# A conformer block with dilated attention: the place of one small DMA read in SyncE's queue

## The chip, the cores and the metric

The kernel runs on one core of one Trainium2 chip. The metric is the device time in microseconds (us) of one execution; the lower the better. Engines are named as the profile names them: PE is TensorE, DVE is VectorE, ACT is ScalarE, POOL is GpSimd, and SP is SyncE, which here does nothing but issue DMAs.

## The reference

One block on a sequence of 1024 tokens of width 1024: a gated convolution branch and an attention branch are mixed by gates and projected, and a feed-forward part with a short convolution follows. Only the attention matters here. Each of the 16 heads attends three times, with windows of 128, 512 and 2048 tokens at dilations 1, 4 and 16, and the three results are mixed by their log-sum-exp:

```python
for window, dilation in DILATION_GROUPS:          # (128, 1), (512, 4), (2048, 16)
    o_g, lse_g = dilated_window_attention(q, k, v, slopes, window, dilation)
    outs.append(o_g)
    lses.append(lse_g)
mix = jax.nn.softmax(jnp.stack(lses), axis=0)
o = jnp.einsum('gbsh,gbshd->bshd', mix, jnp.stack(outs))
```

That is one softmax over all (query, key) pairs with a bias: -slope x distance plus the logarithm of how many of the three windows hold the pair.

## The kernel before, in words

The kernel runs through stages: input norm and convolution branch, query-key-value projection, gate products, the **attention loop**, output projections, feed-forward part. The attention loop takes the stretch from about 590 to 864 us.

**Heads and slots.** A head is eight steps ("places" 0 to 7), two halves of four. Places 0 to 3 score the first 512 queries. Places 4 to 7 score the last 512 queries, in two parts: the *far* keys (more than the near range away, taken by residue modulo 4, place 4) and the *near* keys (query blocks 7, 6, then 4 and 5, at places 5 to 7). A score goes to PSUM (L924, L925, L963), VectorE adds the mask and takes the row's extreme (L928), ScalarE takes the exponential and sums it (L972). Twelve steps later the weights are transposed on PE (`flip`, L1023), split into a high and a low part on ACT and DVE (`ph` L1044, `pl` L1045), and multiplied with the values (`weigh`, L1061, L1062). Between these, PE works on the gate and convolution projections (L120 to L122), which fill its time.

**The statistics.** For the last 512 queries the far part and the near part of a row's softmax are computed apart, in different partition layouts. Each has a pair (extreme, sum) per row, kept in the tile `own[h]`: index 0 on its second axis is near, 1 is far. To join them, each side must see the other's pair in its own layout, in the tile `other[h]`:

- `near_to_far(h)` (L989) copies the near pairs to the far layout, four DMAs of 1 KB from SBUF to SBUF, one for each near query block. Each needs that block's sum.
- `far_out(h)` (L992) writes the far pairs, 4 KB, to a DRAM buffer `dstat[h % 2]`.
- `far_to_near(h)` (L995) reads them back in the near layout, 4 KB. It must wait until the write has landed.
- `compare(h)` (L999) subtracts the two extremes on VectorE. It is the first reader of `other` and needs all five copies. `combine(h)` follows one step later: the common factor (L1005 to L1008) and the scaling of the weights on POOL (L975).

By the program, for head h: `far_out` comes at place 6, `near_to_far` at place 0 of the next head, `far_to_near` at place 1 of the next head, `compare` at place 5 of the next head.

**The loads.** `head(h)` (L741 to L750) loads for one head the queries `q` and the keys `kk` (two DMAs), 512 KB each, and the mask `m`, 320 KB. Each tile has two buffers. `head(h + 2)` is called at place 1 of head h + 1, in the same step as `far_to_near(h)` and before it. `values(h)` loads `v` and `vf`.

**What sets the order.** PE, DVE, ACT and POOL run the loop in the order written (a manual schedule). SyncE is not among them: a scheduler puts its DMAs into one queue by its own estimate of when each is ready. SyncE issues strictly in that order; a DMA that waits holds all behind it. In the order that the scheduler made, the read `far_to_near(h)` stands right behind its write `far_out(h)`, or one DMA later. Outputs that pass through the same queue: `do` (the head's result, L1072), `dgate` and `dya` (L234, L249), and loads of weights and convolution rows `raw_*` (L93).

Of the kernel before, what the change touches and what calls it, by code (L numbers as in the profile page):

```python
# [61 lines left out]
def block_kernel(ctx: ExitStack, tc: tile.TileContext, x, xT, x0, g2, pack, mask,  # L62
                 w_first, w_ch, w_qkv, w_co, w_ao, w_o, w_up, w_down, out):
    nc = tc.nc
    act, dve, pool, pe, sp = nc.scalar, nc.vector, nc.gpsimd, nc.tensor, nc.sync
# [88 lines left out]
    def fetch(dst, src):  # L154
        sp.dma_start(dst.bitcast(F32), src.bitcast(F32))
# [12 lines left out]
    dstat = [dr.tile([P, 4, 2], F32, name=f"dstat{i}") for i in range(2)]  # L168
# [137 lines left out]
    if True:  # L306
# [156 lines left out]
        a, b = range(4), range(4, 8)  # L463
# [269 lines left out]
        def conv_result(c):  # L733
# [4 lines left out]
                           scale=pk[:, C_CG + c : C_CG + c + 1])  # L738
            act.dma_start(da[:, c, :], ordered)

        def head(h):  # L741
            hp, r, g8 = h // 2, (h % 2) * DH, h // 8
            q = p2.tile([P, T], F32R, tag="q", bufs=2, name=f"q_{h}")
            kk = p2.tile([P, 2, T], F32R, tag="kk", bufs=2, name=f"kk_{h}")
            m = p2.tile([P, 640], F32, tag="m", bufs=2, name=f"m_{h}")
            fetch(q, dq[g8].rearrange("p s c t -> (p s) c t")[2 * r : 2 * r + P, hp % 4, :])
            for s in range(2):
                fetch(kk[s:P:2], dk[g8][r : r + DH, :, hp % 4, :])
            sp.dma_start(m, mask[h])
            return q, kk[:, 0], kk[:, 1], m  # L750

        cover(COVER)
# [65 lines left out]
        with tc.manual_schedule(engines=hand):  # L818
# [4 lines left out]
            for n, (a, b) in enumerate(PAIRS):  # L823
# [13 lines left out]
                if n == 3:  # L837
                    tiles[0] = head(0)
# [57 lines left out]
    if True:  # L896
# [84 lines left out]
        own, other, shares = {}, {}, {}  # L981
# [4 lines left out]

        def near_to_far(h):
            for i in range(4):
                sp.dma_start(other[h][32 * i : 32 * i + 32, 1], own[h][:, 0, i])  # L989

        def far_out(h):
            sp.dma_start(dstat[h % 2], own[h][:, 1])  # L992

        def far_to_near(h):
            sp.dma_start(other[h][:, 0], dstat[h % 2].rearrange("(i a) r s -> (a r) i s", i=4))  # L995

        def compare(h):
            f = ready2("both", [P, 2, 4], F32, 2, f"both_{h}")
# [111 lines left out]
        with tc.manual_schedule(engines={ENG.Activation, ENG.DVE, ENG.PE, ENG.Pool}):  # L1110
# [3 lines left out]
            for at in range(len(slots) + BACK + 1):  # L1114
# [4 lines left out]
                if cur is not None:  # L1119
                    h, half, n = cur  # L1120
                    place = at % 8
                    if place == 4:
                        statistics(h)
                    if place == 5:
                        values(h)
                    if place == 1 and h + 1 < H:
                        tiles[h + 1] = head(h + 1)
                    new = score(h, tiles[h], SCORES[half][n])
# [27 lines left out]
                for ago, n0, send in ((2, 0, far_out), (1, 3, near_to_far), (READ, 0, far_to_near)):  # L1156
                    if 0 <= at - ago < len(slots) and slots[at - ago][1:] == (1, n0):
                        send(slots[at - ago][0])
# [343 lines left out]
    if True:  # L1502
# [49 lines left out]
        for f in range(FT):  # L1552
# [12 lines left out]
            r = ready.pop(0)  # L1565
# [15 lines left out]
    with tc.tile_pool(name="ph5", bufs=1, reuse_waits="tile") as p5_:  # L1581
# [31 lines left out]
        def residual(half, n, j):  # L1613
            r = p5_.tile([P, 512], F32, tag="res", bufs=4, name=f"res_{half}_{n}_{j}")
            sp.dma_start(r, dx2[half * 4 + n][:, j * 512 : j * 512 + 512])
            return r
# [107 lines left out]
        for n in range(3):  # L1724
            r = residual(0, n, 1)
# [75 lines left out]
```

## Time and profile before

| | |
|---|---|
| median of 3 runs | 1699.01 us (1698.5 to 1700.75) |
| the profiled execution: its own time | 1695.4 us |
| the profiled execution: span, first to last instruction | 1693.6 us |
| granted TensorE clock | 1.000 |
| attention loop | 590 to 864 us |
| one head in the loop | 16.1 to 18.9 us from one comparison (L999) to the next |

How to read the rows that the prediction shows. A row of the timeline is: start, duration, engine, line, operation, output tile <- input tiles, shape, count, and in brackets the idle time of that engine before it and what ended it. For SyncE (SPq) a row is the issue of a DMA, not its transfer. The view of waits gives total, times and longest. The name of the one that ended a wait is inferred: where several DMAs are waited for, it can name another than the one that came last. The view by windows gives, for a stretch, each engine's busy time, the clock and the DMA engines' share. "DMA to landing" is the time from issue until the data has landed, as minimum, median and maximum of the instructions chosen.

### The profile page before, as it was taken

Reading aid. Unit: us, or ns where it says so; the run is one execution under the profiler, and the core shown is the slowest. Engines: PE = TensorE matmul, PEld = TensorE weight load, DVE = VectorE, ACT = ScalarE, POOL = GpSimd, SP = SyncE. Lnnn points to the kernel's source line nnn. Section 1 sums busy time; section 2 is a strip of 40 time slices with the busy share of each in tenths; the row PEclk is TensorE's granted clock in tenths of the full one; section 3 lists DMA queues with packets and bytes.
Section 4 is the critical chain, followed back from the end, with each engine's and each line's share of the span. In section 5 each row is a group of like instructions: output and inputs, shape, how many; then the busy total and the mean of one; then the engine's idle time right before and its main releaser. Section 6 shows DMA issues by size and latency. Waiting matters only on the chain.

```text
span 1693.6 us, 22622 instructions
## 1 busy us (share of the span) xinstructions
PE 1681.4 (99%) x7939; PEld 1397.1 (82%) x7939; DVE 1303.1 (77%) x2114; ACT 787.9 (47%) x1351; POOL 224.3 (13%) x300
## 2 busy tenths in 40 slices
PE   9999999999999999999999999999999999999999
PEld 7888888888888888888888888888888888888887
DVE  6999999999876567767658654887777677789863
ACT  5411233233245478767646433544544455543431
POOL 0000132033000255555410000000000000000000
PEclk9999999999999999999999999999999999999999
DMA  9411145344555977886769594622222222499851
GB/s 375 153 50 50 50 137 162 125 137 137 175 178 195 320 226 238 261 243 201 221 214 333 187 335 147 227 99 76 75 90 85 87 75 87 145 366 322 287 172 50
DMA packets 187121, 300.24 MB, mean 177 GB/s; under 512 B 32256, under 2 KB 90240, under 8 KB 186496
## 3 DMA queue, kind: packets, MB, share of 16 engines
q1 hardware_dynamic: 185712, 294.48, 52.1%
q10 hardware_dynamic: 1296, 4.33, 0.6%
q8 instruction: 62, 1.02, 0.2%
q14 instruction: 51, 0.42, 0.1%
HBM read 214.74 MB, written 83.95 MB: 176 GB/s over the span
## 4 chain that ended last, share of the span: by engine, by line
PE 92%; DMA 3%; DVE 2%; ACT 1%; issue 1%; SPq 0%; POOL 0%; ACTq 0%; DVEq 0%
PE dx L1607 7%; PE xz L144 6%; PE xz L145 6%; PE xz L146 6%; PE dy L1607 5%; PE qkv L139 5%; PE qkv L137 5%; PE qkv L138 5%; PE y L145 2%; PE y L144 2%; PE y L146 2%; PE pp L1023 2%; PE wo L138 2%; PE wo L139 2%; PE wo L137 2%; PE o L1062 2%
## 5 line engine op out<-in xcount | busy, mean ns | idle before, releaser
L137 PE MATMUL qkv<-hi_qkv,hT 128*128 128x512 f32 x384 | 151.2, 395 | 0.0
L139 PE MATMUL qkv<-hi_qkv,hT 128*128 128x512 f32 x384 | 149.8, 391 | 0.0
L138 PE MATMUL qkv<-lo_qkv,hT 128*128 128x512 f32 x384 | 149.8, 391 | 0.0
L1510 DVE SCALAR_TENSOR_TENSOR u<-u,pk 128x1023 f32<-128x1023 f32 x88 | 112.1, 1275 | 1.2 <-ACT u L1508 0.9
L113 POOL TENSOR_TENSOR rs<-ss,mhalf 128x8 f32<-128x8 f32 x32 | 66.3, 2074 | 294.0 <-DVE ss L112 294.0
L1045 DVE TENSOR_TENSOR pl<-pp,ph 128x512 fp32r<-128x512 f32 (+1 forms) x95 | 58.7, 618 | 46.7 <-ACT ph L1044 46.5
L586 DVE SCALAR_TENSOR_TENSOR cacc<-csum,both,cacc 128x512 f32<-128x512 f32 x120 | 89.4, 745 | 0.3
L586 DVE SCALAR_TENSOR_TENSOR cacc<-apad,pk,cacc 128x512 f32<-128x512 f32 x120 | 88.2, 745 | 0.0
L89 DVE TENSOR_TENSOR lo_uv<-raw_uv,hi_uv 128x1024 fp32r<-128x1024 f32 x20 | 24.5, 1226 | 79.4 <-ACT hi_uv L88 79.4
L139 PEld LDWEIGHTS qkv<-hi_qkv,hT 128*128 128x128 f32 x384 | 72.1, 188 | 15.0
L586 DVE SCALAR_TENSOR_TENSOR codd<-apad,pk,codd 128x513 f32<-128x513 f32 x112 | 83.7, 748 | 0.7 <-ACT codd L579 0.7
L138 PEld LDWEIGHTS qkv<-lo_qkv,hT 128*128 128x128 f32 x384 | 72.2, 188 | 14.3
L137 PEld LDWEIGHTS qkv<-hi_qkv,hT 128*128 128x128 f32 x384 | 72.1, 188 | 14.2
L928 DVE CUSTOM_DVE_ANT_0 p<-s,m 128x512 f32<-128x512 f32 (+1 forms) x120 | 59.1, 502 | 17.2 <-POOL pf L975 6.3
L1044 ACT ACTIVATE ph<-pp 128x512 fp32r<-128x512 f32 (+1 forms) x95 | 51.5, 542 | 43.9 <-PE pp L1023 43.1
L144 PE MATMUL xz<-h2left,hi_uv 128*128 128x512 f32 x176 | 68.6, 390 | 0.0
L144 PE MATMUL xz<-blk_t,hi_s3g 128*128 128x512 f32 x176 | 68.6, 390 | 0.0
L146 PE MATMUL xz<-h2left,lo_uv 128*128 128x512 f32 x176 | 68.5, 389 | 0.0
L145 PE MATMUL xz<-h2left,hi_uv 128*128 128x512 f32 x176 | 68.5, 389 | 0.0
L145 PE MATMUL xz<-blk_t,hi_s3g 128*128 128x512 f32 x176 | 68.5, 389 | 0.0
L146 PE MATMUL xz<-blk_t,lo_s3g 128*128 128x512 f32 x176 | 68.5, 389 | 0.0
L1508 ACT ACTIVATE u<-u,pk 128x1024 f32<-128x1024 f32 x44 | 54.5, 1239 | 9.5 <-DVE u L1497 4.5
(479 smaller groups left out, 5056.5 us busy)
## 6 DMA issues: line engine op xcount, KB each, us to landing
wr<-w_down SPq DMA_DIRECT2D x45, 512.0 KB, 5.9
kk<-dk SPq DMA_DIRECT2D x32, 512.0 KB, 6.1
gr<-dff SPq DMA_DIRECT2D x62, 256.0 KB, 5.4
raw_qkv<-w_qkv SPq DMA_DIRECT2D x24, 512.0 KB, 4.9
dff<-u SPq DMA_DIRECT2D x22, 512.0 KB, 2.6
raw_uv<-w_up SPq DMA_DIRECT2D x21, 512.0 KB, 3.7
raw_ug<-w_up SPq DMA_DIRECT2D x20, 512.0 KB, 3.6
dv<-v SPq DMA_DIRECT2D x16, 512.0 KB, 2.8
```

Source lines behind the costliest of these rows:

```text
L113: pool.tensor_tensor(out=dst, in0=tmp, in1=mhalf[:, : tmp.shape[1]], op=ALU.pow)
L137: pe.matmul(ps, ah, hi[:, k % 2, :], start=(k == 0), stop=False)
L138: pe.matmul(ps, ah, lo[:, k % 2, :], start=False, stop=False)
L139: pe.matmul(ps, al, hi[:, k % 2, :], start=False, stop=(k == KT - 1))
L144: pe.matmul(o, wh[:, k, :], bh[:, k, :], start=(start and k == 0), stop=False, skip_group_check=not start)
L145: pe.matmul(o, wh[:, k, :], bl[:, k, :], start=False, stop=False, skip_group_check=not start)
L146: end = pe.matmul(o, wl[:, k, :], bh[:, k, :], start=False, stop=(k == 3), skip_group_check=not start)
L586: dve.scalar_tensor_tensor(out=out_, in0=src[:, i : i + size], scalar=w(i), in1=out_, op0=ALU.mult, op1=ALU.add)
L928: dve.tensor_tensor_reduce(out=pt, in0=s, in1=m, scale=-1.0, scalar=3e38, op0=ALU.add, op1=ALU.min, accum_out=nm)
L1045: dve.tensor_tensor(out=runs(pl[:, c]), in0=order(pp[:, c]), in1=runs(ph[:, c]).bitcast(F32), op=ALU.subtract)
L1510: dve.scalar_tensor_tensor(out=acc[:, d:], in0=src[:, : T - d], scalar=w(2 - d), in1=acc[:, d:], op0=ALU.mult, op1=ALU.add)
L1607: pe.matmul(banks[n][:, cols], a[:, c], b[:, d], start=(start and i == 0 and m == 0), stop=(stop and i == nf - 1 and m == 2), skip_group_c ...
```

## The change

```diff
@@ inside block_kernel @@
+        queued = []
+
         def head(h):
...
             fetch(q, dq[g8].rearrange("p s c t -> (p s) c t")[2 * r : 2 * r + P, hp % 4, :])
             for s in range(2):
                 fetch(kk[s:P:2], dk[g8][r : r + DH, :, hp % 4, :])
-            sp.dma_start(m, mask[h])
+            queued[:] = [sp.dma_start(m, mask[h])]
             return q, kk[:, 0], kk[:, 1], m
...
         def near_to_far(h):
             for i in range(4):
-                sp.dma_start(other[h][32 * i : 32 * i + 32, 1], own[h][:, 0, i])
+                queued[:] = [sp.dma_start(other[h][32 * i : 32 * i + 32, 1], own[h][:, 0, i])]
...
         def far_to_near(h):
-            sp.dma_start(other[h][:, 0], dstat[h % 2].rearrange("(i a) r s -> (a r) i s", i=4))
+            with tc.issue_after(queued[0].ins):
+                sp.dma_start(other[h][:, 0], dstat[h % 2].rearrange("(i a) r s -> (a r) i s", i=4))
```

`queued` holds the last DMA that the program wrote among the masks and the near copies. `issue_after` tells the scheduler to put the read behind it in SyncE's queue. For heads 0 to 13 that is the mask of head h + 2; for heads 14 and 15, which have no such load behind them, it is the near copy of block 7 (i = 3), which the scheduler issues first of the four. The order on PE, DVE, ACT and POOL is the same row for row; only SyncE's differs, and line numbers move by two or three. In head 0 the read stood behind the mask before, too.

SyncE's queue at head 11, before. `own_11` and `other_11` are the head's statistics, `q_13`, `kk_13` and `m_13` the loads of the next head but one; the last two numbers are rows and elements, and x2 stands for two DMAs:

```order
L992 DMA dstat1_140<-own_11_7392 128x8
L249 DMA dya2_102<-ya_2_1_7432 128x512
L995 DMA other_11_7393<-dstat1_140 128x4x2
L989 DMA other_11_7393<-own_11_7392 32x4x2 x2
L155 DMA q_13_7548<-dq1_75 128x1024
L155 DMA kk_13_7549<-dk1_77 64x2x1024
L1072 DMA do_108<-ot_10_0_7518 128x512
L989 DMA other_11_7393<-own_11_7392 32x4x2 x2
L155 DMA kk_13_7549<-dk1_77 64x2x1024
L749 DMA m_13_7550<-mask 128x640
L155 DMA vf_12_7689<-dv1_79 128x4x128
```

The same place of the changed kernel:

```order
L994 DMA dstat1_140<-own_11_7392 128x8
L249 DMA dya2_102<-ya_2_1_7432 128x512
L991 DMA other_11_7393<-own_11_7392 32x4x2 x2
L155 DMA q_13_7548<-dq1_75 128x1024
L155 DMA kk_13_7549<-dk1_77 64x2x1024
L1075 DMA do_108<-ot_10_0_7518 128x512
L991 DMA other_11_7393<-own_11_7392 32x4x2 x2
L155 DMA kk_13_7549<-dk1_77 64x2x1024
L751 DMA m_13_7550<-mask 128x640
L998 DMA other_11_7393<-dstat1_140 128x4x2
L155 DMA vf_12_7689<-dv1_79 128x4x128
```

The read moved past nine DMAs, from two rows behind its write to behind the mask; nothing else moved. Heads 1 to 13 differ in this way.

SyncE's queue at head 14, before, where no load of a later head follows:

```order
L992 DMA dstat0_139<-own_14_8128 128x8
L249 DMA dya6_106<-ya_6_0_8183 128x512
L995 DMA other_14_8129<-dstat0_139 128x4x2
L989 DMA other_14_8129<-own_14_8128 32x4x2 x2
L1072 DMA do_108<-ot_13_0_8250 128x512
```

and of the changed kernel:

```order
L994 DMA dstat0_139<-own_14_8128 128x8
L249 DMA dya6_106<-ya_6_0_8183 128x512
L991 DMA other_14_8129<-own_14_8128 32x4x2
L998 DMA other_14_8129<-dstat0_139 128x4x2
L991 DMA other_14_8129<-own_14_8128 32x4x2
L1075 DMA do_108<-ot_13_0_8250 128x512
```

Here the read moved past one near copy. Head 15 differs in the same way.

## The prediction

> **What bounds the kernel now.** I read the page first, then the stage that the change touches.
>
> ```profile
> span 1693.6 us, 22622 instructions
> PE 1681.4 (99%) x7939; PEld 1397.1 (82%) x7939; DVE 1303.1 (77%) x2114; ACT 787.9 (47%) x1351; POOL 224.3 (13%) x300
> ```
>
> TensorE sets the time: whatever doesn't move PE moves nothing. So the question is how much PE idles in the attention loop (590 to 864 us) because of SyncE's queue. The view by windows, columns span, busy time of PE, PEld, DVE, ACT and POOL, granted clock, DMA share and GB/s:
>
> ```profile
> 590.00:692.00 102.00, 101.09 (x595) 85.92 (x594) 75.31 (x268) 80.55 (x234) 52.67 (x88) 1.00 0.80 242
> 692.00:829.00 137.00, 132.56 (x787) 112.52 (x786) 95.68 (x333) 100.18 (x290) 70.09 (x115) 1.00 0.77 230
> 829.00:864.00 35.00, 34.67 (x205) 29.55 (x204) 19.12 (x62) 20.70 (x56) 12.38 (x23) 1.00 0.59 180
> ```
>
> PE idles 0.91 + 4.44 + 0.33 = 5.68 us in the loop, most of it in heads 6 to 13. No change to this queue can win more than that and what stretched matmuls hide. The waits of the loop, SyncE's own queue first, then VectorE's for DMA (total, times, longest):
>
> ```profile
> SPq L995 <- DMA dstat<-own: 68.7, 15, 5.4
> ...
> DVE both L999 <- DMA kk<-dk: 4.4, 4, 2.0
> DVE p L928 <- DMA m<-mask: 3.2, 1, 3.2
> ...
> DVE both L999 <- DMA raw_a<-da: 0.8, 1, 0.8
> DVE both L999 <- DMA other<-own: 0.8, 1, 0.8
> ```
>
> SyncE stands 68.7 us in 15 waits, 4.6 us each, before the read of the far rows' statistics (L995), until their write has landed. VectorE waits 6.0 us at the comparison (L999) and 3.2 us for a mask. I take the three names at L999 for one thing: the last of the copies into `other`. One head shows why. SyncE's queue for head 11 (start, duration):
>
> ```profile
> 777.56 0.39 SPq L992 DMA_DIRECT2D dstat<-own  x1
> 778.04 0.45 SPq L249 DMA_DIRECT2D dya<-ya  x1
> 783.33 0.37 SPq L995 DMA_DIRECT2D other<-dstat  x1
> 783.79 1.26 SPq L989 DMA_DIRECT2D other<-own  x2
> 785.16 0.53 SPq L155 DMA_DIRECT2D q<-dq  x1
> ...
> 787.01 1.53 SPq L989 DMA_DIRECT2D other<-own  x2
> 788.60 0.59 SPq L155 DMA_DIRECT2D kk<-dk  x1
> 789.24 0.58 SPq L749 DMA_DIRECT2D m<-mask  x1
> ```
>
> From 778.49 to 783.33 nothing is issued: 4.84 us. What stands behind was ready: the matmul and the accumulation that release the `q` load and the last two near copies are
>
> ```profile
> 776.35 0.28 PE L925 MATMUL s<-kk,q 128*128 128x256 f32 x1
> ...
> 779.03 0.19 ACT L972 ACTIVATION_READ_ACCUMULATOR p<-p,own 128x1 f32 x1
> ```
>
> so `q` could go at 776.6 and went at 785.16; the near copies could go at 779.2 and went at 787.0 and 787.7. From issue to landing, the last two near copies, then the statistics' write, then the mask of this head took
>
> ```profile
> DMA to landing us min/median/max: 5.0/5.3/5.5
> ...
> DMA to landing us min/median/max: 5.8/5.8/5.8
> ...
> DMA to landing us min/median/max: 6.5/6.5/6.5
> ```
>
> so the near copies landed at 792.5 and 792.7, and VectorE's comparison started at once:
>
> ```profile
> 792.78 0.17 DVE L999 TENSOR_TENSOR both<-own,other 128x8 f32<-128x8 f32 x1 [0.79 <-DMA other<-own]
> ```
>
> **The change, part by part.** No instruction is added or removed; PE, DVE, ACT and POOL keep their order. In heads 1 to 13 the read goes from right behind its write to behind the second `kk` load and the mask. Head 0 is unchanged; in heads 14 and 15 the read only goes behind the first near copy.
>
> *The hold.* In head 11 the first near copies follow at 778.6 instead of 783.79: 5.2 us earlier, and so do `q` (779.96), the last near copies (781.8), `kk` and `m` (784.0), all later than their releases. The read goes out at 784.7, after its write has landed (777.56 + 5.8 = 783.4), so it waits no more. In earlier heads the queue lags less and the gain is smaller, but there the comparison waits for nothing that matters.
>
> *The landings.* Issues move 5.2 us; landings move less, for the DMA engines were still emptying. Windows over the hold of head 11:
>
> ```profile
> 778.50:783.30 4.80, 4.80 (x32) 3.90 (x31) 2.73 (x8) 3.45 (x11) 4.80 (x9) 1.00 0.77 254
> 783.30:786.50 3.20, 3.20 (x21) 2.83 (x21) 2.81 (x9) 2.70 (x8) 2.36 (x4) 1.00 0.22 14
> ```
>
> The unused share is 0.23 x 4.80 + 0.78 x 3.20 = 3.6 us. I take 3.6 us as the shift (bounds: 2.5, the hole at 0.22 alone, and 5.2). The last near copy then lands at 789.1 and the mask, which landed 6.5 us after 789.24 (795.7), at 792.1. The read is one small copy behind it. What it costs to stand there shows in the issues of 4 KB and 1 KB (KB each, median us to landing):
>
> ```profile
> other<-own SPq DMA_DIRECT2D x64, 1.0 KB, 4.2
> other<-dstat SPq DMA_DIRECT2D x16, 4.0 KB, 1.9
> ```
>
> The read has 1.9 because the hold had drained the queue; the tiny near copies have 4.2, and 5.0 to 5.5 right behind `q` and `kk`. So I let the read land in order, about 0.2 us after the mask: 792.3. Without its wait the comparison would come at 792.78 - 0.79 = 791.99. A wait of 0.3 stays of 0.79.
>
> [...]
>
> *What PE gets back.* The idle times that follow such waits: PE's rows first, then the comparison of head 12, a group of transposes of head 7 beside a normal one, the same place of head 6 as the first row's of head 7, and the transposes of head 11:
>
> ```profile
> 731.58 0.50 PE L1062 MATMUL o<-pl,v 128*128 128x512 f32 x1 [1.07 <-DVE pl L1045]
> ...
> 760.60 0.47 PE L924 MATMUL s<-kk,q 128*128 128x512 f32 x1 [0.55 <-DMA kk<-dk]
> ...
> 764.34 0.33 PE L1062 MATMUL o<-pl_far,vf 128*128 128x128 f32 x1 [0.38 <-DVE pl_far L1045]
> ...
> 777.05 0.39 PE L1062 MATMUL o<-pl,v 128*128 128x256 f32 x1 [0.30 <-DVE pl L1045]
> ...
> 813.26 0.39 PE L1062 MATMUL o<-pl,v 128*128 128x256 f32 x1 [1.71 <-DVE pl L1045]
> ...
> 811.29 0.17 DVE L999 TENSOR_TENSOR both<-own,other 128x8 f32<-128x8 f32 x1 [2.04 <-DMA kk<-dk]
> ...
> 725.38 1.07 PE L1023 MATMUL pp_far<-ident,pf 128*128 128x128 f32 x4
> ...
> 743.73 0.62 PE L1023 MATMUL pp_far<-ident,pf 128*128 128x128 f32 x4
> ...
> 699.77 0.39 PE L1062 MATMUL o<-pl,v 128*128 128x256 f32 x1 [0.38 <-DVE pl L1045]
> ...
> 795.80 1.07 PE L1023 MATMUL pp_far<-ident,pf 128*128 128x128 f32 x4
> ```
>
> Head 12: 1.71. Head 10: 0.30. Late loads of head 11: 0.55 + 0.38. At 731.58 I count 1.07 less 0.38, which the same place loses in head 6 (699.77) after a wait too short to matter: 0.69. Two groups of transposes, stretched because POOL's scaling came late, lose 1.07 - 0.62 = 0.45 each: 0.90. Sum: 1.71 + 0.30 + 0.93 + 0.69 + 0.90 = 4.53 us. I give back 0.6 for waits of a few tenths that the late read leaves, estimated from one group of transposes and a little more: **3.9 us faster**.
>
> Against the profiled execution (span 1693.6, its own time 1695.4) this is a span of 1689.7. The runs' median is 1699.01, 3.6 us above that execution; I carry the difference over: 1699.0 - 3.9 = **1695.1**. A difference under 0.2%, 3.4 us, I count as no change that this kernel's measurement can tell; the three runs alone spread over 2.25 us.
>
> **The rivals.**
>
> *Hidden anyway.* The read replaces the near copies as the last input. It lands 795.7 - 792.6 + 0.2 = 3.3 us behind the last near copy, because the second `kk` and the mask are between them. If the landings shift by just that, the comparison waits as long as before, and only the mask's wait goes: 0.93 us, 1698.1. For: a shift of 3.6 is an estimate, its lower bound is 2.5. Against: with the hole filled, each head begins with less queued from the one before, so later heads should shift more.
>
> *The late read wins: slower.* Place: VectorE's comparison, behind which the residues of the flips (L1045) and the score minima (L928) queue, and PE behind them. It decides where the shift is below 3.3 us in the late heads. With 1.7, the read lands 1.6 us later than the near copies did. Eight heads (6 to 13) would wait 1.6 more, and PE pays 1.71 / 2.04 = 0.84 for each: 8 x 1.6 x 0.84 = 10.8, less 0.9 for the mask: 1708.9. Against: the hole alone is worth 2.5.
>
> [...]
>
> *Not what it says.* SyncE might stand as long behind another wait, a buffer's release or an output tile. Then nothing moves: 1699.0. The releases of head 11 speak against it.
>
> **How the numbers follow.** Forecast 0.55, hidden 0.22, late read 0.13, overtaking 0.05, not what it says 0.05. The forecast's own range is 1693.5 to 1697.0, so it gives 0.42 to faster and 0.13 to the same; overtaking gives 0.05 to faster; hidden gives 0.02 faster, 0.19 same and 0.01 slower; not what it says gives 0.05 to the same; the late read gives 0.13 to slower. Faster 0.49, same 0.37, slower 0.14. The range goes from 1692.0, where all of the loop's idle 5.68 and the 0.90 of the transposes were won (1692.4), to 1701.0, which takes in the hidden case, no effect, and the mild third of the late read.
>
> **What the changed profile would show.** SyncE's wait for `dstat<-own` falls from 15 times and 68.7 us to two or three. The hole in DMA share before the near copies is gone. The read takes 5 to 8 us to land instead of 1.9. The comparison's waits fall from 6.0 to under 2 us and the mask's wait is gone; PE's idle in 692 to 829 falls from 4.44 to about 1.5. I am wrong if the comparison waits longer than before with the read as its last input, or if SyncE's hold reappears under another name, or if PE's gaps stay although those waits are gone.

## The result, and the profile after

| | median us | lowest to highest | runs |
|---|---|---|---|
| before | 1697.34 | 1693.84 to 1700.75 | 6 |
| changed | 1690.43 | 1689.68 to 1692.42 | 6 |

The ratio is 0.9962, with a 95% interval of 0.9947 to 0.9976: the change makes the kernel faster by 0.24 to 0.53%. The forecast was 1695.1 and its range began at 1692.0, so direction and mechanism were right and the size was not. The profiled execution after took 1690.27 us with a span of 1688.5, which is 5.1 less than the 1693.6 before.

The page after, its first part:

```profile
span 1688.5 us, 22626 instructions
PE 1679.1 (99%) x7939; PEld 1398.0 (83%) x7939; DVE 1303.0 (77%) x2114; ACT 786.5 (47%) x1351; POOL 225.2 (13%) x300
```

The view by windows after, over the same three stretches (columns span, busy time of PE, PEld, DVE, ACT, POOL, granted clock, DMA share, GB/s):

```profile
590.00:692.00 102.00, 101.09 (x594) 85.84 (x593) 75.39 (x268) 80.17 (x234) 52.42 (x88) 1.00 0.84 254
692.00:829.00 137.00, 135.53 (x815) 116.30 (x813) 98.70 (x347) 103.28 (x301) 74.27 (x123) 1.00 0.80 236
829.00:864.00 35.00, 34.91 (x207) 29.70 (x205) 17.71 (x54) 19.43 (x48) 12.43 (x24) 1.00 0.40 122
```

PE's idle in heads 6 to 13 falls from 4.44 to 1.47 us, and in the whole loop from 5.68 to 2.47. The waits after, SyncE's queue for the statistics and VectorE's comparison (total, times, longest):

```profile
SPq L998 <- DMA dstat<-own: 2.8, 2, 2.1
...
DVE both L1002 <- DMA raw_a<-da: 0.9, 1, 0.9
```

Of SyncE's 68.7 us in 15 waits 2.8 us in two are left. VectorE's waits for the mask are gone, and so are those for copies into `other` in heads 1 to 15. The 0.9 us that are left, named `raw_a`, are head 0's: its comparison starts 0.08 us after its own read has landed, before and after, and that read's place did not change. SyncE's queue of head 11 after (start, duration), then that head's comparison:

```profile
775.62 0.53 SPq L155 DMA_DIRECT2D q<-dq  x1
776.25 1.44 SPq L155 DMA_DIRECT2D kk<-dk  x1
777.77 0.54 SPq L1075 DMA_DIRECT2D do<-ot  x1
778.41 1.31 SPq L991 DMA_DIRECT2D other<-own  x2
779.77 0.63 SPq L155 DMA_DIRECT2D kk<-dk  x1
780.46 0.63 SPq L751 DMA_DIRECT2D m<-mask  x1
781.13 0.61 SPq L998 DMA_DIRECT2D other<-dstat  x1
```

```profile
789.48 0.16 DVE L1002 TENSOR_TENSOR both<-own,other 128x8 f32<-128x8 f32 x1
```

then the landings of this mask and of this read:

```profile
DMA to landing us min/median/max: 6.7/6.7/6.7
...
DMA to landing us min/median/max: 6.3/6.3/6.3
```

and the view of DMA issues for all sixteen reads (KB each, median us to landing):

```profile
other<-dstat SPq DMA_DIRECT2D x16, 4.0 KB, 5.7
```

There is no hole among these rows. The mask lands at 780.46 + 6.7 = 787.2, the read 0.2 us behind it at 781.13 + 6.3 = 787.4, and the comparison runs at 789.48: the read has 2.1 us to spare, and VectorE waits for nothing. The `q` load goes 785.16 - 775.62 = 9.5 us earlier than before, which is more than one hold of 4.84 us. The same holds in the other late heads: in the kernel before, the comparisons of heads 6 to 8 and 10 to 13 start 0.08 us after the last near copy has landed; in the changed kernel all of heads 6 to 13 have 5 us or more between the two.

Where PE got it back is seen by the same matmul in both traces. The one that stood at 813.26 before, behind 1.71 us of idle, after:

```profile
808.65 0.28 PE L1065 MATMUL o<-pl,v 128*128 128x256 f32 x1
```

4.61 us earlier, with no gap. All of the 5.1 us come from the loop: the same comparison of start times gives 0.5 us at the transposes of head 7, 1.3 at 759, 1.9 at 775, 4.6 at 808 and 5.3 at 826 (times after); after 864 about 0.5 is given back, where the end of head 15 waits longer for `pl`.

### The profile page after: what moved, and what is told of

Read it like the earlier page. It is cut to its first block, busy times and chain, and to the rows that moved or that the text cites. A ratio compares the mean times of both kernels' runs of the same rounds, so it can differ in the third digit from the quotient of the medians.

```text
span 1688.5 us, 22626 instructions
## 1 busy us (share of the span) xinstructions
PE 1679.1 (99%) x7939; PEld 1398.0 (83%) x7939; DVE 1303.0 (77%) x2114; ACT 786.5 (47%) x1351; POOL 225.2 (13%) x300
## 4 chain that ended last, share of the span: by engine, by line
PE 96%; DMA 1%; ACT 1%; DVE 1%; issue 1%; POOL 0%; SPq 0%; ACTq 0%; DVEq 0%; POOLq 0%
PE dx L1610 7%; PE xz L144 6%; PE xz L146 6%; PE xz L145 6%; PE dy L1610 5%; PE qkv L137 5%; PE qkv L139 5%; PE qkv L138 5%; PE y L146 2%; PE y L145 2%; PE y L144 2%; PE pp L1026 2%; PE wo L139 2%; PE wo L137 2%; PE wo L138 2%; PE o L1065 2%
```

## The experiments

Each ran beside the kernel before on the same chip; ratios are to those runs.

### The hold kept, by a read that nobody uses

```diff
         def far_to_near(h):
+            idle = p2b.tile([P, 4, 2], F32, tag="idle", bufs=2, name=f"idle_{h}")
+            sp.dma_start(idle, dstat[h % 2].rearrange("(i a) r s -> (a r) i s", i=4))
             with tc.issue_after(queued[0].ins):
                 sp.dma_start(other[h][:, 0], ...)
```

> The changed kernel's order, with a second read of the same statistics put back right behind their write, into a tile that nothing reads; so SyncE stands until the write has landed, as before, while the read that the comparison uses stays behind the mask. If the hold is the whole cause: the gain is gone, time within 0.1% of the kernel before (0.999 to 1.002), SyncE's wait for the write about 65 us in 13 to 15 waits again, the comparison's waits 6 us or more. If the place of the read that is used were the cause (out of the way of the near copies): 0.996 of the kernel before, as the change.

Measured: 1700.39 us (1699.23 to 1703.01, 8 runs), 1.0025 [1.0015, 1.0035]. The new order without the end of the hold is slower than before, and about 10 us slower than the changed kernel. Its waits, SyncE's and VectorE's:

```profile
SPq L998 <- DMA dstat<-own: 59.9, 15, 5.9
...
DVE both L1004 <- DMA other<-dstat: 12.7, 8, 3.5
```

So the hold's end is what wins, and the new place without it wins nothing. That the place is not needed for the gain is shown by no_readback below, which has no hold and the old place. The time is above the 0.999 to 1.002 that I had allowed: with the queue held, the read becomes the last input of the comparison, just as the rival "the late read wins" had it (in heads 5 to 12 the comparison starts within 0.2 us of its landing). Whether the extra read by itself, 0.4 us of SyncE's time in each head, has a part in the loss is not shown. A part of the loss in this profile is a fallen clock (0.50 for 6.8 us), which the last section tells.

### The change in heads 6 to 13 alone, and in heads 1 to 5 alone

```diff
-            with tc.issue_after(queued[0].ins):
+            with (tc.issue_after(queued[0].ins) if 6 <= h < 14 else ExitStack()):
```

and, for the other, `if h < 6`.

> The change in heads 6 to 13 alone; heads 0 to 5, 14 and 15 as before. If PE loses its time to the hold in the late heads alone, as the profile's rows say: the whole gain, 0.996 (0.995 to 0.997) of the kernel before. If a queue that lags is built up head by head from the first one on: less, 0.997 to 0.999.

Measured: 1690.59 (1690.07 to 1690.90, 6 runs), 0.9966 [0.9954, 0.9978]: all of the gain, though SyncE still waits seven times for a write. One wait for the read came up, 1.2 us in head 6, which begins with what the holds of heads 1 to 5 left in the queue.

> The change in heads 1 to 5 alone; the others as before. If only the late heads pay: no change, 0.9995 to 1.0005. If the lag is built up from the first head on: 0.997 to 0.999, with the comparison's waits in heads 6 to 8 gone and those of heads 10 to 12 back.

Measured: 1692.17 (1691.24 to 1696.93, 10 runs), 0.998 [0.9971, 0.9989], with ten such waits left: more than half of the gain, from heads in which nothing had waited. VectorE's waits, in heads 12, 11 and 0:

```profile
DVE both L1002 <- DMA kk<-dk: 1.5, 1, 1.5
DVE both L1002 <- DMA other<-own: 0.8, 1, 0.8
DVE both L1002 <- DMA other<-dstat: 0.4, 1, 0.4
```

Against the 1696.48 of the kernel before, the late heads alone win 5.9 us and the early heads alone 4.3: together far more than the two at once. They win the same thing twice, and the issue times of the `q` load say what (starts from the timelines, us):

| `q` load queued in | before | heads 1 to 5 alone | heads 6 to 13 alone | all heads |
|---|---|---|---|---|
| head 5 | 677.3 | 672.0 | 679.0 | 671.9 |
| head 6 | 696.9 | 693.9 | 693.7 | 690.0 |
| head 11 | 785.2 | 782.8 | 776.4 | 775.6 |
| head 12 | 803.2 | 799.9 | 793.0 | 792.2 |

With holds in heads 1 to 5, the load of head 5 goes 5 to 7 us late. With holds only from head 6 on, the lag starts from nothing at head 5 and is 3.9 us at head 6 and 7.2 at head 11. Where the holds end at head 6, 3.7 us are left there and 0.8 at head 11. So a hold was not paid in its own head: it lengthened a lag that the next heads began with, and most of PE's idle in the kernel before, 4.44 of the loop's 5.68 us, lay in heads 6 to 13, where the lag was longest.

### One hold, in head 11

```diff
-            with tc.issue_after(queued[0].ins):
+            with (ExitStack() if h == 11 else tc.issue_after(queued[0].ins)):
```

> The change in all heads but head 11, whose read stands right behind its write again, so SyncE is held once, for some 5 us. Theory (the lag that holds leave in the queue is carried from head to head, and one hold by itself finds the queue early enough): 1690.0 to 1691.2, SyncE's wait for dstat 3 or 4 times and under 9 us, the comparison's waits for other under 1 us. Rival (each hold pays for itself, as my prediction counted: 1.71 and 0.93 us of PE behind the hold of head 11): 1692.5 to 1693.5, with PE gaps of 0.5 to 1.7 us between 760 and 815.

Measured: 1691.25 (1690.10 to 1691.87, 5 runs), 0.9962 [0.9948, 0.9975], 0.05 above what the theory allowed. SyncE waits for a write fewer times than I had expected, and the comparison's 1.0 us is again head 0's. Its waits, and its `q` loads of heads 11 and 12:

```profile
SPq L998 <- DMA dstat<-own: 4.5, 2, 3.0
...
DVE both L1002 <- DMA other<-dstat: 1.0, 1, 1.0
```

```profile
778.29 0.53 SPq L155 DMA_DIRECT2D q<-dq  x1
...
792.44 0.53 SPq L155 DMA_DIRECT2D q<-dq  x1
```

The load of head 11 goes 2.7 us later than in the changed kernel (775.62), that of head 12 only 0.2 (792.21): one hold is made up within one head. The hold is also shorter than in the kernel before, 3.0 us against 4.84, for the write landed 3.9 us after its issue instead of 5.8. PE has the same gaps as after, none above 0.1 us between 732 and 864. In my sum the hold of head 11 cost 2.6 us; alone, and so shortened, it costs nothing on PE. The profiled execution is 1.6 us longer than the changed kernel's, but that lies at 897 and 1465, far behind the loop.

### The read's place: no read from DRAM, one load later, two loads later

The copy taken from SBUF where the old read stood, with no write to wait for:

```diff
-            with tc.issue_after(queued[0].ins):
-                sp.dma_start(other[h][:, 0], dstat[h % 2].rearrange("(i a) r s -> (a r) i s", i=4))
+            with tc.issue_after(written[h].ins):
+                sp.dma_start(other[h][:, 0], own[h][:, 1])
```

> The far rows' copy into other is taken from own in SBUF, right behind the write, where the old read stood, and waits for no write. It leaves out the change of layout (near rows get the far rows' numbers in the wrong places). Theory (all of the loss was the hold, and a read that stands behind the mask lands in time and costs nothing): as the changed kernel, 1690.4 within 0.8, SyncE's wait for dstat gone altogether, no wait of VectorE's at the comparison for other. Rival (the late read gives back the 0.6 us of my prediction): 1689.8 or less, and PE idle in 692 to 829 at 0.9 instead of 1.47.

Measured: 1690.96 (1690.26 to 1691.49, 8 runs), 0.9964 [0.9953, 0.9976]; span 1688.4. Not waiting at all is worth no more than waiting behind the mask: the give-back of 0.6 us that I took off does not exist. With hold_kept this makes all four cases: held with the read early (the kernel before) or late (hold_kept) is slow, not held with the read early (this run) or late (the changed kernel) is fast.

For the next two, `queued` holds the next far-`v` or the next `v` load in place of the mask, and the read is written behind it:

```diff
-            fetch(vf, ...)
+            queued[:] = [fetch(vf, ...)]
...
-            sp.dma_start(m, mask[h])
...
+                        if h:
+                            far_to_near(h - 1)
```

> The change, with the read one load later still: behind the next vf load (256 KB) instead of the mask. In the changed kernel's head 11 and 12 the read landed 2.1 and 3.3 us before the comparison; one load later it is issued 0.7 and 2.2 us later and lands behind another 256 KB. Theory (that slack is real and in order of landing): 1690.4 to 1692.0, the comparison waits under 3 us in all, PE idle in 692 to 829 at 1.5 to 2.5. Rival (the read's place is already at the edge): 1693 or more.

Measured: 1690.85 (1689.94 to 1693.38, 11 runs), 0.9969 [0.996, 0.9978]; no wait for `other`, PE's idle in 692 to 829 is 1.49. The slack of about 2 us is real, and most of it is used up in some heads: in heads 1 to 13 the read lands 0.3 to 4.2 us before its comparison, against 1.7 to 4.6 in the changed kernel.

> The change, with the read far later: behind the next v load. In the changed kernel v is issued 4.5 us (head 11) and 5 us (head 12) behind the read; the read would then land about 791 and 807.5 at the earliest, 1.5 and 1.1 us past the comparison of those heads. Theory (SyncE's hold is gone, so what is lost here is the price of a late read by itself): 8 late heads with a wait of 1 to 3 us, 8 to 24 us at the comparison, and half of each on PE (in hold_kept 13.7 us of such waits went with 7.05 us more PE idle than in the changed kernel): 1695 to 1703. Rival (a copy as small as this lands ahead of the loads before it): under 1692.

Measured: 1709.72 (1708.99 to 1710.44, 4 runs), 1.0078 [1.0062, 1.0095]. Slower by 13 us than before and by 19 than the changed kernel; I had expected 1703 at most. VectorE's waits at the comparison:

```profile
DVE both L1002 <- DMA other<-dstat: 12.1, 8, 2.5
DVE both L1002 <- DMA other<-own: 6.4, 3, 2.9
DVE both L1002 <- DMA do<-ot: 1.9, 1, 1.9
DVE both L1002 <- DMA dstat<-own: 1.6, 1, 1.6
```

22.0 us in 13 heads, early ones too, and a span 20.0 us longer than after. In heads 1 to 14 the comparison starts within 0.2 us of the read's landing, whatever name the wait has. So the read's place costs nothing up to the far-`v` load and 19 us behind the `v` load that follows. Nothing here shows a small copy overtaking the loads ahead of it: with the queue held for a write only once, for 1.7 us, the read still takes 5.2 us to land in the median. My price of half a us of PE for each us of such wait came from idle time alone (hold_kept's 7 us against 13.7) and was too low, because PE is also busy for longer: 1685.6 us here against 1679.1 in the changed kernel. The 13.7 had also taken in 1.0 us of head 0, whose comparison waits for its read in every kernel that has it. By spans the price is 20.0 / 22.0 = 0.91 here and (1701.2 - 1688.5) / 12.7 = 1.00 there.

### Both kernels again, and three more profiles of the kernel before

> The kernel before, once more, for a second profile and more times. If the median of 1699 against 1695.4 for the profiled execution is a constant of the measurement: the new times keep to one value per chip within 2 us, and PE's idle time in the loop is 5.7 us again. If the waits on DMAs differ from execution to execution: its times spread over 5 us or more, wider than the 2.7 us of the changed kernel, and PE's idle time in the loop differs by more than 1 us between the two profiles. Ratio 1.000 either way.

> The changed kernel as it is, for a second profile and its spread, beside the kernel before. Theory (SyncE's hold delayed every load behind it, the lag of the queue grew head by head, and the waits that follow from it differ from execution to execution): 1690.4, within 1689.5 to 1692.5 in all runs; the kernel before again spreads over 5 us or more, 1693.8 to 1701, with its median near 1696.5; PE idle in 590 to 864 again about 2.5 us and at the same places, where two profiles of the kernel before had theirs at different places. Rival (the before's first profile was only one of several, and the change has as wide a spread): a spread of 4 us or more and the gaps at other places.

> The kernel before, one more profiled execution. Theory (its spread of 7 us over 48 runs lies in how long VectorE's comparisons wait for the statistics): the span lies 0.8 to 1.0 us above 1688.4 for each us that the comparisons wait for other, so an execution of 1695 has 5 to 6 us of such waits and one of 1698 or more has 8 us or more. Rival (the spread lies elsewhere): 5 to 6 us of waits whatever the time.

> As before_p1: the span is 1688.4 plus 0.8 to 1.0 times the comparisons' waits for other (raw_a left out); the rival has 5 to 6 us of waits whatever the time.

> As before_p1: the span is 1688.4 plus 0.8 to 1.0 times the comparisons' waits for other (raw_a left out); the rival has 5 to 6 us of waits whatever the time.

| execution | time us | span | waits for `other` at the comparison, without head 0 | for a mask (L928) |
|---|---|---|---|---|
| before, first profile | 1695.40 | 1693.6 | 5.2 | 3.2 |
| before_again | 1695.17 | 1693.4 | 5.9 | none |
| before_p1 | 1696.84 | 1695.1 | 7.4 | 3.4 |
| before_p2 | 1697.56 | 1695.8 | 6.6 | 3.1 |
| before_p3 | 1699.04 | 1697.3 | 6.4 | 4.8 |
| changed | 1690.27 | 1688.5 | 0 | none |
| change_again | 1690.01 | 1688.2 | 0 | none |

One sign failed: PE's idle in the loop was to differ by more than 1 us between the first two profiles of the kernel before, and it is 5.7 and 5.9 us; only the three later ones (7.7, 7.1 and 7.2) differ so. before_again's eleven runs have a median of 1696.28, 0.9998 [0.9987, 1.0008]; change_again's five have 1690.14, 0.9964 [0.995, 0.9978]. In all, the kernel before has a median of 1696.77 over its 71 runs and spreads from 1693.84 to 1701.08. The changed kernel has 1690.27 over 11 runs, from 1689.68 to 1692.42; its two profiles have their gaps at the same places. In the five profiles of the kernel before, the loss against the changed one's is 5.1, 4.9, 6.6, 7.3 and 8.8 us, and by the start of the same matmuls nearly all of it arises between 640 and 830, but split over the heads in another way each time: 0, 3.6, 1.4, 1.4 and 3.7 us at head 6, and 2.0, 1.0, 1.7, 1.1 and 1.5 at head 12. So the spread does lie in the loop. My rule of 0.8 to 1.0 us of span for each us of wait holds for three of the five (1.0, 0.85, 0.91); before_p2 has 1.1 and before_p3 1.4, and the 8 us that I asked of an execution above 1698 are not there. In before_p3 a part is something else. Its comparison of head 6 and PE behind it:

```profile
708.26 0.17 DVE L999 TENSOR_TENSOR both<-own,other 128x8 f32<-128x8 f32 x1 [2.89 <-DMA kk<-dk]
...
709.67 0.39 PE L1062 MATMUL o<-pl,v 128*128 128x256 f32 x1 [2.00 <-DVE pl L1045]
```

(in the first profile the same comparison waited 0.33 us), and the windows of the same execution, the granted clock being the third number from the end:

```profile
710.00:711.00 1.00, 1.00 (x7) 0.87 (x6) 0.83 (x5) 0.73 (x2) 0.77 (x3) 1.00 0.99 362
711.00:712.00 1.00, 1.00 (x5) 0.77 (x5) 0.29 (x1) 0.85 (x4) 1.00 (x3) 0.57 1.08 375
712.00:713.00 1.00, 1.00 (x6) 1.00 (x5) 0.41 (x2) 0.47 (x1) 1.00 (x3) 0.50 1.13 344
713.00:714.00 1.00, 1.00 (x4) 0.80 (x3) 0.84 (x2) 0.83 (x3) 1.00 (x3) 0.50 1.11 409
714.00:715.00 1.00, 1.00 (x4) 0.72 (x4) 0.40 (x3) 0.00 (x0) 1.00 (x2) 0.72 1.05 404
```

One wait of 2.9 us made a gap of 2.00 us, and behind the gap PE ran at half its clock for some 3 us: 0.43 + 0.50 + 0.50 + 0.28 = 1.7 us more, on a PE that is shown as fully busy. That is 3.7 us from one late copy, and by the start of the same matmuls 3.6 us arise there that the first profile does not have; before_p3 is 1697.3 - 1693.6 = 3.7 us longer than it. before_again had the same gap (1.99) at the same head and the same fall of the clock, and fewer waits elsewhere.

## Why the prediction was right in its course and wrong in its size

**Right.** SyncE's hold was the cause (hold_kept: keep it, and the gain is gone; no_readback: end it and leave the copy where it was, and the gain is there). The waits fell as forecast: the hold to two waits, the comparison's under 2 us, the mask's to none, PE's idle in heads 6 to 13 to about 1.5 us. The read landed 5.7 us after its issue (the median), inside the 5 to 8 forecast, and 0.2 us behind the mask.

**The rival "overtaking".** The prediction gives it a chance of 0.05: the read would land ahead of the loads issued before it. No run shows that. In heads 0 to 13 of the changed kernel the read landed 0.2 to 0.3 us behind the DMA issued ahead of it, and of the 252 DMAs that SyncE issues there in the loop, and of the 249 in the kernel before, none landed ahead of one issued before it. So by every row of these two profiles small copies landed in order.

**Wrong: the constant 3.6 us.** The step that failed most is "the runs' median is 1699.01, 3.6 us above that execution; I carry the difference over". It was no constant. It was the same loss as the one being removed, in executions where it was larger, as far as five profiles show it; before_p3, at 1699.04, shows such a one: one longer wait in head 6 (2.9 us) and a halved clock (0.50) behind it. Three runs also were too few: the median over 71 is 1696.77. Of the 4.7 us between 1695.1 and 1690.43, 2.2 are this starting point (1699.01 - 1696.77). A further 1.2 are the first profile's luck (the medians differ by 6.3 us, the profiled pair by 5.1). The range's low end, 1692.0, was counted from the same 1699.01, and so shut out what came.

**Wrong: the sum of 3.9 against the profiled pair's 5.1.** The other 1.2 us, by its terms:

- 1.71 (head 12), 0.30 (head 10) and 0.55 + 0.38 (late loads of head 11): won, no such gap is left.
- 0.69 at 731.58: not won. The gap is still there, behind VectorE's own work:

```profile
728.36 2.01 DVE L185 TENSOR_TENSOR aT<-raw_a,aT 128x512 fp32r<-128x512 f32 x1 [0.47 <-ACT aT L192]
...
731.02 0.50 PE L1065 MATMUL o<-pl,v 128*128 128x512 f32 x1 [1.05 <-DVE pl L1048]
```

  The split of `aT` takes 2.01 us ahead of the residue that PE waits for. I had put a gap down to the comparison because it had the releaser of the others.
- 0.90 for two stretched groups of transposes: mostly not won. They are still

```profile
724.99 0.93 PE L1026 MATMUL pp_far<-ident,pf 128*128 128x128 f32 x4
...
793.20 0.94 PE L1026 MATMUL pp_far<-ident,pf 128*128 128x128 f32 x4
```

  against 1.07, so 0.27 in all.
- The 0.6 given back for a late read: nothing (no_readback gains none).
- Not in the sum at all: 5.3 us were won by 826, and the terms that held make 1.71 + 0.30 + 0.93 + 0.27 = 3.2. The other 2.1 are a gap of 0.22 at 831.54, which I had left out, and matmuls and transposes, most of them shorter by a tenth or two, which no list of gaps shows. About 0.2 net went again at the end of the loop and behind it.

A shorter way was open. The comparison's waits for `other` were 6.0 - 0.8 = 5.2 us, and the spans differ by 5.1: in this pair the whole wait counted, and not only what PE's gaps show of it. It is no exact rule: over the five profiles the loss is 0.85 to 1.4 us for each us of wait.

**The landings.** The shift of 3.6 us (bounds 2.5 to 5.2) was too small: the mask landed at 787.2 instead of 795.7, 8.5 us earlier. Of the 9.5 us by which the `q` load moved, 1.9 are PE's own gain by then, so the queue caught up 7.6 us in head 11. I had counted that head's hold (4.84) and not the lag that earlier heads left, although the rival "hidden anyway" names the reason in its "against". That is why the late read, priced by a shift of 1.7 to 3.6, cost nothing: hidden anyway and the late read both needed a queue that stays late, as in hold_kept.

## What to carry to other kernels

In SyncE's queue here the lag went from one head to the next: in head 11, whose own hold was 4.84 us, the queue caught up 7.6 us once no head held it. On a queue that runs behind, count the lag from the first iteration. Where a kernel's runs spread over more than its profile explains, ask whether the spread is the loss that the change removes before adding it to the forecast as a constant. The small copy that must wait for a write cost nothing here behind large loads while it landed 0.3 us or more before its reader (read_behind_far_v), and 19 us one load later (read_behind_v); such a last safe place can be found by moving the copy a load at a time, with its landing read against its reader at each step.

## What the runs showed of the chip that I had not expected

Some gaps of about 2 us went with a halved clock of TensorE. In the fourteen profiles, PE's gaps in the loop of 1.99 (before_again and read_behind_v), 2.00 (before_p3) and 3.13 us (hold_kept) each went with a granted clock of 0.50, and the others, of up to 1.71 us, with 1.00, as did one of 1.94 at 872 in the kernel with heads 1 to 5 changed. The half clock lasted 3.4 us in the first three (in before_p3 from 711.15 to 714.56) and 6.8 in hold_kept. Four cases do not show that the length of the gap alone decides. hold_kept's gap, and the windows behind it:

```profile
819.18 0.58 PE L1067 MATMUL o<-pl,v 128*128 128x256 f32 x1 [3.13 <-DVE pl L1050]
```

```profile
819.00:820.00 1.00, 0.82 (x4) 0.82 (x5) 0.93 (x7) 0.88 (x3) 0.27 (x1) 0.50 0.29 92
...
824.00:825.00 1.00, 1.00 (x4) 0.77 (x3) 1.00 (x4) 0.57 (x2) 1.00 (x2) 0.53 1.00 213
825.00:826.00 1.00, 1.00 (x9) 0.82 (x7) 0.14 (x3) 0.00 (x0) 1.00 (x2) 1.00 0.79 289
```

There the clock fell within the gap and stayed at half for nearly 6 us behind it, so a gap of 3.1 us cost about 6. What the four cases show is that the loss had a step in it: beside its own length such a gap cost 1.7 us (before_p3) to 2.9 us (hold_kept, half of the nearly 6), and that part stands in the profile as busy time.
